# A Hymba layer with sixteen experts on one core: g3 split, the last up product in two banks, one scatter at the end

## The chip, the cores and the metric

The kernel runs on one core of one Trainium2 chip. Its time is device microseconds (us) of that core, taken as the median of several runs. One further execution was recorded by the hardware profiler; the rows below come from it.

## What is computed

One layer for 512 tokens of width 1024, all in float32. An attention part (latent attention and differential attention side by side) comes first; then each token goes to two of sixteen experts, which lie inside one group of four. The change concerns the experts only:

```python
D_MODEL, SEQ, N_EXPERTS, D_EXPERT = 1024, 512, 16, 512
def _hmoe(h, w_rg, b_rg, w_re, b_re, w_gate, w_up, w_down):
    t = h.reshape(B * S, D)
    g_logits = (t @ w_rg + b_rg).astype(jnp.float32)
    g_idx = jnp.argmax(g_logits, axis=-1)
...
    y = jnp.zeros_like(t)
    for e in range(N_EXPERTS):
        he = jax.nn.silu(t @ w_gate[e]) * (t @ w_up[e])
        y = y + gate[:, e:e + 1] * (he @ w_down[e])
    return y.reshape(B, S, D)

...
        x = x + g2 * _hmoe(h2, w_rg[l], b_rg[l], w_re[l], b_re[l], w_gate[l], w_up[l], w_down[l])
```

`gate` holds a token's weight for each expert, zero for those that it did not choose; `h2` is x after normalisation and modulation.

## The kernel before

**Tiles.** Each expert works on 128 slots, filled with the tokens that chose it. Its rows are gathered from DRAM by an indirect DMA on GpSimd's queue (`xg`, line 1602), worked on, weighted by the gate and added to the output by an indirect DMA that adds in DRAM (`scatter`, line 1609). If an expert has more tokens than slots, a second program part, which lies behind a branch, does the rest; it was not entered in the profiled execution.

**Chunks.** An expert's three weight matrices are cut into twelve chunks of 128 partitions x 1024 values: g0 to g3 (gate) and u0 to u3 (up), each with two of the eight k tiles of 128 and 512 columns, and d0 to d3 (down), each one k tile with 1024 columns. The list `CH` sets their order. The gate chunks run one expert ahead: u0 to u3 of expert e, g0 to g3 of e + 1, d0 to d3 of e, and so on. The weights come in loads of 1 MB, two chunks each, into an arena of twelve places (`PLACES`); the next load into a place is issued when both of its chunks are used.

**Split and whole chunks.** Most products take operands of the type fp32r. To keep float32's precision a chunk is split into two such parts four chunks ahead of its use (`AHEAD`): ScalarE casts it to `whi` (line 1579), VectorE takes the rest as `wlo` (line 1580). `mm3` (lines 235 to 237) then adds three products, whi by xh, wlo by xh and whi by xl. A split chunk is six such narrow products of 512 columns. A chunk for which `whole` is true isn't split: it is multiplied in float32 (line 1901), which is two products, recorded as four matmuls, and costs neither ScalarE nor VectorE anything. In the kernel before these are g3 and u3 of each expert. A split normally stands ahead of the products of the chunk four before it; where the table `late_split` names that chunk, it stands behind them.

**Turns.** The gathered rows of an expert have to be transposed. `turn(e, q)`, for half q of the eight k tiles, is four transposes on TensorE (line 1710, into `ps_tp`), four scaled copies `xf` and one cast `xh` on ScalarE (lines 1695 and 1697) and the rest `xl` on VectorE (line 1698). In the kernel before, the first half of expert e stands behind g3 of expert e - 1, which is just ahead of d0 of expert e - 2, and the second behind u0 of expert e - 1. The indirect DMA for expert e + 2's rows is issued behind the second. `turn_act` does the same for the activation: `sl` is the gate through Silu, multiplied by the up product on VectorE (line 1927), transposed on TensorE (line 1870), copied to `he` on ScalarE (line 1873), its rest taken on VectorE (line 1874). It stands behind g1 of the next expert. One expert needs the two turns and one `turn_act`: three times four transposes.

**Slots.** A chain of small steps per expert (`slot_chain`) finds its tokens' row numbers: a one-hot `oh` on VectorE (line 1658), four bf16 products on TensorE, five tiny VectorE operations (lines 1633 to 1640). Numbers in the loop over the chunks say at which chunk each step is issued.

**Order.** The program's order is kept on each engine as it is written; an engine that has to wait holds up all that stands behind it. `take` and `drop` hand out and return buffers.

**The last expert.** Its down products are done for the first 512 output columns, chunk by chunk; those for the second 512 are put off, then made in one go. Each half of `y` has a scatter of its own, over the output seen as half rows, with row numbers `i0` and `i1`. `y` is line 1962: gate, times the PSUM bank `ps_sc`, times the row vector g2.

## Time and profile before

| | us |
|---|---|
| runs | 679.75, 676.32, 678.45 |
| median of the runs | 678.45 |
| the profiled execution's own time | 679.67 |
| its span, first to last instruction | 678.0 |
| TensorE, matmuls (PE) | 639.6 busy, 94% |
| TensorE, weight loads (PEld) | 505.5 busy, 75% |
| VectorE (DVE) | 554.9 busy, 82% |
| ScalarE (ACT) | 433.3 busy, 64% |
| GpSimd (POOL) | 157.9 busy, 23% |

Busy times are shares of the span. Matmuls follow each other in a pipeline, and their ends are modelled: the duration of one matmul is longer than the distance to the next, so TensorE's pace is read from the starts of its instructions. The same holds in part for VectorE, where the start of the next instruction is a little ahead of the recorded end. The expert loop fills the span from about 360 us to its end. The 1.67 us by which the profiled execution's own time exceeds its span lie outside the recorded instructions.

### The profile page before, as it was taken

How to read it: one execution, taken by the hardware profiler on the slowest of the kernel's cores; microseconds unless marked ns; L12 is line 12 of the kernel's file. 1: busy time of each engine (PE TensorE's matmuls, PEld its weight loads, DVE VectorE, ACT ScalarE, POOL GpSimd, SP SyncE). 2: the span in 40 equal slices, each digit the busy share in tenths (PEclk: the TensorE clock that was granted, in tenths of full speed). 3: DMA queues.
4: the chain of work that ended last, by engine and by line, in shares of the span. 5: the costliest groups of instructions: out<-in, count | busy, mean ns of one | idle time of the engine just before them, and what ended most of it. 6: DMA issues, size and time to landing. Idle time of an engine off the chain costs nothing.

```text
span 678.0 us, 10463 instructions
## 1 busy us (share of the span) xinstructions
PE 639.6 (94%) x3465; PEld 505.5 (75%) x3465; DVE 554.9 (82%) x1229; ACT 433.3 (64%) x835; POOL 157.9 (23%) x230
## 2 busy tenths in 40 slices
PE   8998899999989999999999999999999999999991
PEld 7666798998777876767787677777777777777761
DVE  5768887898887677789988888998988888888870
ACT  6575555755664454433477877777787778777750
POOL 2653021266120001132010111222211022231121
...
DMA packets 61931, 169.67 MB, mean 250 GB/s; under 512 B 8807, under 2 KB 23629, under 8 KB 54576
## 3 DMA queue, kind: packets, MB, share of 16 engines
...
q14 instruction: 31, 0.25, 0.1%
...
## 4 chain that ended last, share of the span: by engine, by line
PE 53%; DVE 10%; DMA 3%; ACT 2%; issue 2%; POOL 0%; POOLq 0%; DVEq 0%; ACTq 0%
PE ps_mm L1901 8%; PE ps_mm L235 7%; PE ps_mm L237 7%; PE ps_mm L236 7%; PE ps_sc L235 4%; PE ps_sc L237 4%; PE ps_sc L236 4%; PE ps_tp L1710 2%; DVE acc L1238 2%; DMA xg<-h_d,idx 1%; PE ps_po L887 1%; PE ps_sc L860 1%; PE ps_tp L1870 1%; PE ps_sc L1088 1%; PE ps_tp L874 1%
## 5 line engine op out<-in xcount | busy, mean ns | idle before, releaser
L1580 DVE TENSOR_TENSOR wlo<-wraw,whi 128x1024 fp32r<-128x1024 f32 (+1 forms) x168 | 190.3, 1170 | 8.9 <-ACT whi L1579 8.8
L1579 ACT CAST whi<-wraw 128x1024 fp32r<-128x1024 f32 (+1 forms) x168 | 157.9, 1005 | 0.9 <-PE ps_sc L237 0.5
L1609 POOL DMA_INDIRECT out_dram<-y,idx x15 | 39.9, 2659 | 216.3 <-DVE y L1962 216.3
L235 PE MATMUL ps_mm<-whi,xh 128*128 128x512 f32 x192 | 84.3, 439 | 0.0
L237 PE MATMUL ps_mm<-whi,xl 128*128 128x512 f32 x192 | 75.4, 393 | 0.0
L236 PE MATMUL ps_mm<-wlo,xh 128*128 128x512 f32 x192 | 75.0, 391 | 0.0
L1901 PE MATMUL ps_mm<-wraw,xf 128*128 128x512 f32 x128 | 60.2, 592 | 0.0
L1695 ACT ACTIVATE xf<-ps_tp,norm2x 128x128 f32<-128x128 f32 x120 | 45.1, 462 | 18.2 <-PE ps_tp L1710 18.2
L235 PE MATMUL ps_mm<-whi,hT_hi 128*128 128x256 f32 x192 | 56.7, 295 | 0.0
L236 PE MATMUL ps_mm<-wlo,hT_hi 128*128 128x256 f32 x192 | 55.0, 287 | 0.6 <-DVE wlo L223 0.6
L237 PE MATMUL ps_mm<-whi,hT_lo 128*128 128x256 f32 x192 | 54.8, 285 | 0.0
L235 PE MATMUL ps_sc<-whi,he 128*128 128x512 f32 x128 | 52.8, 412 | 0.7 <-ACT he L1873 0.7
L1238 DVE SCALAR_TENSOR_TENSOR acc<-adaw,s_c,acc 128x512 f32<-128x512 f32 x60 | 47.0, 791 | 4.6 <-DMA adaw<-in_w_ada_dram 3.8
L237 PE MATMUL ps_sc<-whi,he 128*128 128x512 f32 x128 | 50.2, 392 | 0.0
L236 PE MATMUL ps_sc<-wlo,he 128*128 128x512 f32 x128 | 49.9, 390 | 0.0
L236 PEld LDWEIGHTS ps_mm<-wlo,xh 128*128 128x128 f32 x192 | 36.2, 189 | 9.8 <-issue 3.3
L235 PEld LDWEIGHTS ps_mm<-whi,xh 128*128 128x128 f32 x192 | 36.1, 188 | 9.7 <-issue 3.6
L237 PEld LDWEIGHTS ps_mm<-whi,xl 128*128 128x128 f32 x192 | 36.0, 188 | 8.3
L236 PEld LDWEIGHTS ps_mm<-wlo,hT_hi 128*128 128x128 f32 x192 | 37.3, 194 | 1.0 <-DVE wlo L223 0.9
L235 PEld LDWEIGHTS ps_mm<-whi,hT_hi 128*128 128x128 f32 x192 | 37.3, 194 | 0.3
L1873 ACT CAST he<-ps_tp 128x512 fp32r<-128x512 f32 x16 | 9.4, 587 | 43.7 <-PE ps_tp L1870 43.7
L237 PEld LDWEIGHTS ps_mm<-whi,hT_lo 128*128 128x128 f32 x192 | 37.2, 194 | 0.0
...
## 6 DMA issues: line engine op xcount, KB each, us to landing
...
```

The lines of the kernel that those rows point to most:

```text
L235: PE.matmul(o, xh, wh, start=first, stop=False)
L236: PE.matmul(o, xh, wl, start=False, stop=False)
L237: PE.matmul(o, xl, wh, start=False, stop=last)
L860: PE.matmul(s_[:, z * W:(z + 1) * W], qT[h // 4][0:QK + NT, h % 4, qs], kT[h // 4][0:QK + NT, h % 4, 0:W], start=True, stop=True)
L1238: V.scalar_tensor_tensor(acc[0], w[:, z, :], sc, acc[0], op0=OP.mult, op1=OP.add)
L1579: A.copy(hi[:, s], src)
L1580: V.tensor_tensor(lo[:, s], src, f32(hi[:, s]), op=OP.subtract)
L1609: G.indirect_dma_start(out=o, out_offset=bass.IndirectOffsetOnAxis(ap=idx[:, :1], axis=0), in_=y[:, cs], in_offset=None, compute_op=OP.add)
L1695: A.activation(xf[:, kk, :], p3[:, kk, :], AF.Identity, scale=gc, bias=sc)
L1710: PE.transpose(pt[:, kk * P:(kk + 1) * P], xs_["g"][:, e % 2, k0:k0 + P], ident)
L1873: A.copy(xs_["he"][:, 0], p3)
L1901: PE.matmul(eb[nm, e], eb["xf", e][:, 2 * j + kk - 4, :], src, start=(j == 0 and kk == 0), stop=(j == 3 and kk == 1))
```

## The change

`whole` is true for u3 alone: g3 is split like the other chunks, so each expert has eleven split chunks where it had ten. Three tables move with it. `late_split` names u3, d1, g1 and u0. The first turn of expert e stands behind d2 of expert e - 2, three chunks later than before, and the second behind u2 of expert e - 1, two chunks later. The slot chain starts one chunk later, and its last two steps stand two chunks later than before.

For the last expert the up product goes into two PSUM banks of 256 columns each: u0 to u2 as narrow products of 256 columns, u3 as four float32 products of 256. Then each half is multiplied into `sl` (line 1931 of the new kernel), and `turn_act` runs once for each half, with two transposes each. The last expert's down products are made like all others, both halves of the columns chunk by chunk, and one scatter writes whole rows; the row numbers `i0` and `i1` go.

The new kernel's line numbers differ by a few: `oh` is line 1648, the turn's `xl` line 1688, its transposes line 1700, the activation's transposes line 1860, its `he` lines 1864 and 1865, the whole u3 line 1892 and line 1897 for the last expert, the scatter line 1606.

```diff
@@ whole @@
-        return nm + str(j) in ('g3', 'u3')
+        return nm + str(j) in ('u3',)
...
@@ scatter @@
-    def scatter(idx, y, half=None):
-        o, cs = out, slice(0, D)
-        if half is not None:
-            o, cs = out.rearrange("s (h n) -> (s h) n", h=2), slice(half * 512, half * 512 + 512)
-        G.indirect_dma_start(out=o, out_offset=bass.IndirectOffsetOnAxis(ap=idx[:, :1], axis=0), in_=y[:, cs],
+    def scatter(idx, y):
+        G.indirect_dma_start(out=out, out_offset=bass.IndirectOffsetOnAxis(ap=idx[:, :1], axis=0), in_=y[:],
                              in_offset=None, compute_op=OP.add)
...
@@ turn_act @@
-    def turn_act(e):
+    def turn_act(e, lo=0, hi=4):
 
         sl = eb["sl", e]
         pt = take("tp")
-        for kk in range(4):
-            PE.transpose(pt[:, kk * P:(kk + 1) * P], sl[:, kk * P:(kk + 1) * P], ident)
-        drop(sl)
-        p3 = pt.rearrange("p (k n) -> p k n", k=4)
-        A.copy(xs_["he"][:, 0], p3)
-        V.tensor_tensor(xs_["he"][:, 1], p3, f32(xs_["he"][:, 0]), op=OP.subtract)
+        for kk in range(lo, hi):
+            PE.transpose(pt[:, (kk - lo) * P:(kk - lo + 1) * P], sl[:, kk * P:(kk + 1) * P], ident)
+        if hi == 4:
+            drop(sl)
+        p3 = pt[:, 0:(hi - lo) * P].rearrange("p (k n) -> p k n", k=hi - lo)
+        A.copy(xs_["he"][:, 0, lo:hi], p3)
+        V.tensor_tensor(xs_["he"][:, 1, lo:hi], p3, f32(xs_["he"][:, 0, lo:hi]), op=OP.subtract)
         drop(pt)
...
-    late_split = {'u3': 1, 'g2': 1, 'g1': 1, 'd3': 1, 'd1': 1, 'g0': 1}
+
+    late_split = {'u3': 1, 'd1': 1, 'g1': 1, 'u0': 1}
...
@@ the loop over the chunks @@
-            d = c - max(12 * e1 - 38, e1 - 2)
+            d = c - max(12 * e1 - 37, e1 - 2)
             if d == 0:
                 ahead[e1] = slot_chain(e1)
-            for _ in range({0: 3, 3: 1, 4: 1}.get(d, 0)):
+            for _ in range({0: 3, 4: 1, 5: 1}.get(d, 0)):
                 next(ahead[e1], None)
-            if e1 == 2 and d == 4:
+            if e1 == 2 and d == 5:
...
         if whole(nm, j):
             for kk in range(2):
                 src = hi[:, kk * 512:kk * 512 + 512] if hi is lo else (hi, lo)[kk]
-                PE.matmul(eb[nm, e], eb["xf", e][:, 2 * j + kk - 4, :], src, start=(j == 0 and kk == 0), stop=(j == 3 and kk == 1))
+                if (nm, e) != ("u", NE - 1):
+                    PE.matmul(eb[nm, e], eb["xf", e][:, 2 * j + kk - 4, :], src, start=False, stop=(kk == 1))
+            if (nm, e) == ("u", NE - 1):
+                for h, u in enumerate(eb[nm, e]):
+                    for kk in range(2):
+                        src = hi[:, kk * 512:kk * 512 + 512] if hi is lo else (hi, lo)[kk]
+                        PE.matmul(u[:, 0:256], eb["xf", e][:, 2 * j + kk - 4, :], src[:, h * 256:h * 256 + 256], start=False,
+                                  stop=(kk == 1))
...
-                eb[nm, e] = take("mm")
+                eb[nm, e] = [take("mm"), take("mm")] if (nm, e) == ("u", NE - 1) else take("mm")
             for kk in range(2):
                 kt = 2 * j + kk
                 cs = slice(kk * 512, kk * 512 + 512)
+                if (nm, e) == ("u", NE - 1):
+                    for h, u in enumerate(eb[nm, e]):
+                        ch = slice(kk * 512 + h * 256, kk * 512 + h * 256 + 256)
+                        mm3(u[:, 0:256], xs_["h"][:, e % 2, kt, :], xs_["l"][:, e % 2, kt, :], hi[:, ch], lo[:, ch], kt == 0, False)
+                    continue
                 mm3(eb[nm, e], xs_["h"][:, e % 2, kt, :], xs_["l"][:, e % 2, kt, :], hi[:, cs], lo[:, cs], kt == 0, kt == 7)
...
-            for n in range(2) if e + 1 < NE else (0,):
+            for n in range(2):
                 cs = slice(n * 512, n * 512 + 512)
                 mm3(eb["y", e][n], xs_["he"][:, 0, j, :], xs_["he"][:, 1, j, :], hi[:, cs], lo[:, cs], j == 0, j == 3)
-            if e + 1 == NE:
-                last.append((hi, lo))
-        if not whole(nm, j) and (nm, e) != ("d", NE - 1):
+        if not whole(nm, j):
...
-        if (nm, j) == ("u", 3):
+        if (nm, j) == ("u", 3) and e + 1 < NE:
             V.tensor_tensor(eb["sl", e], eb["sl", e], eb["u", e], op=OP.mult)
             drop(eb["u", e])
-            if e + 1 == NE:
-                turn_act(e)
+        elif (nm, j) == ("u", 3):
+            for h, u in enumerate(eb["u", e]):
+                V.tensor_tensor(eb["sl", e][:, h * 256:h * 256 + 256], eb["sl", e][:, h * 256:h * 256 + 256], u[:, 0:256],
+                                op=OP.mult)
+                turn_act(e, 2 * h, 2 * h + 2)
+            drop(*eb["u", e])
         for q in range(2):
-            for e1 in (1,) if e < 1 else (e, e + 1, e + 2):
+            for e1 in (e, e + 1, e + 2):
                 if e1 >= NE or e1 < 1:
                     continue
-                at = ((0, "u", 1 + q)) if e1 == 1 else ((e1 - 1, 'g', 3), (e1 - 1, 'u', 0))[q]
+                at = ((0, "u", 1 + q)) if e1 == 1 else ((e1 - 2, 'd', 2), (e1 - 1, 'u', 2))[q]
...
-                if e + 1 == NE and n:
-                    scatter(slots[e][2], y, 0)
-                    for k, (hi, lo) in enumerate(last):
-                        mm3(eb["y", e][n], xs_["he"][:, 0, k, :], xs_["he"][:, 1, k, :], hi[:, cs], lo[:, cs], k == 0, k == 3)
                 V.scalar_tensor_tensor(y[:, cs], eb["y", e][n], slots[e][1], rows["g2"][:, cs], op0=OP.mult,
                                        op1=OP.mult)
             drop(*eb["y", e])
-            if e + 1 == NE:
-                scatter(slots[e][3], y, 1)
-            else:
-                scatter(slots[e][0], y)
+            scatter(slots[e][0], y)
```

VectorE, one expert in the steady loop, before, from the product `sl` behind u3 on. The `wlo` rows are, in order, those of d0, d1, d2, d3 and of the next expert's u0 to u2; `sv` begins the small slot operations.

```order
L1927 TENSOR_TENSOR sl_6797<-sl_6797,ps_mm_6875 128x512
L1580 TENSOR_TENSOR wlo_6934<-wraw_6596,whi_6933 128x1024
L1874 TENSOR_TENSOR he_5431<-ps_tp_6943,he_5431 128x512
L1580 TENSOR_TENSOR wlo_6951<-wraw_6596,whi_6950 128x1024
L1658 TENSOR_TENSOR oh_6956<-iota_307,rkp 128x512
L1580 TENSOR_TENSOR wlo_6965<-wraw_6614,whi_6964 128x1024
L1580 TENSOR_TENSOR wlo_6969<-wraw_6614,whi_6968 128x1024
L1698 TENSOR_TENSOR xl_5430<-xf_6985,xh_5429 128x512
L1580 TENSOR_TENSOR wlo_6993<-wraw_6661,whi_6992 128x1024
L1580 TENSOR_TENSOR wlo_7016<-wraw_6661,whi_7015 128x1024
L1580 TENSOR_TENSOR wlo_7022<-wraw_6742,whi_7021 128x1024
L1633 COPY sv_1333_7025<-ps_po_7004 128x5
```

The same engine and place in the changed kernel. The `wlo` rows are those of g3, d0, d1, d2, d3 and of u0 to u2.

```order
L1927 TENSOR_TENSOR sl_6861<-sl_6861,ps_mm_6935 128x512
L1580 TENSOR_TENSOR wlo_6991<-wraw_6620,whi_6990 128x1024
L1580 TENSOR_TENSOR wlo_6997<-wraw_6650,whi_6996 128x1024
L1865 TENSOR_TENSOR he_5437<-ps_tp_7013,he_5437 128x512
L1580 TENSOR_TENSOR wlo_7021<-wraw_6650,whi_7020 128x1024
L1580 TENSOR_TENSOR wlo_7027<-wraw_6666,whi_7026 128x1024
L1580 TENSOR_TENSOR wlo_7037<-wraw_6666,whi_7036 128x1024
L1648 TENSOR_TENSOR oh_7042<-iota_307,rkp 128x512
L1580 TENSOR_TENSOR wlo_7053<-wraw_6700,whi_7052 128x1024
L1580 TENSOR_TENSOR wlo_7071<-wraw_6700,whi_7070 128x1024
L1580 TENSOR_TENSOR wlo_7077<-wraw_6798,whi_7076 128x1024
L1688 TENSOR_TENSOR xl_5436<-xf_7091,xh_5435 128x512
```

Behind `sl` two `wlo` stand ahead of `he` where one stood; `oh` stands behind two more of them, and the first half's `xl` has moved from behind d3's `wlo` to behind that of u2.

TensorE at the end of the gate chunks of a steady expert, before: the second half of g2, g3 whole (`x2`), the first turn of the next gathered rows, and d0 with `he`.

```order
L235 MATMUL ps_mm_7642<-whi_7625,xh_5429 128x512
L236 MATMUL ps_mm_7642<-wlo_7626,xh_5429 128x512
L237 MATMUL ps_mm_7642<-whi_7625,xl_5430 128x512
L1901 MATMUL ps_mm_7642<-wraw_7334,xf_7603 128x512 x2
L1710 MATMUL ps_tp_7696<-ident,xg_5312 128x128 x4
L235 MATMUL ps_sc_7712<-whi_7649,he_5431 128x512
L236 MATMUL ps_sc_7712<-wlo_7650,he_5431 128x512
L237 MATMUL ps_sc_7712<-whi_7649,he_5431 128x512
L235 MATMUL ps_sc_7713<-whi_7649,he_5431 128x512
L236 MATMUL ps_sc_7713<-wlo_7650,he_5431 128x512
```

The same place in the changed kernel: the second half of g2, the six products of g3, and the first of d0.

```order
L235 MATMUL ps_mm_7933<-whi_7893,xh_5435 128x512
L236 MATMUL ps_mm_7933<-wlo_7894,xh_5435 128x512
L237 MATMUL ps_mm_7933<-whi_7893,xl_5436 128x512
L235 MATMUL ps_mm_7933<-whi_7923,xh_5435 128x512
L236 MATMUL ps_mm_7933<-wlo_7924,xh_5435 128x512
L237 MATMUL ps_mm_7933<-whi_7923,xl_5436 128x512
L235 MATMUL ps_mm_7933<-whi_7923,xh_5435 128x512
L236 MATMUL ps_mm_7933<-wlo_7924,xh_5435 128x512
L237 MATMUL ps_mm_7933<-whi_7923,xl_5436 128x512
L235 MATMUL ps_sc_7987<-whi_7929,he_5437 128x512
L236 MATMUL ps_sc_7987<-wlo_7930,he_5437 128x512
L237 MATMUL ps_sc_7987<-whi_7929,he_5437 128x512
```

Where the two float32 products stood, six narrow ones stand, and the turn is gone from between g3 and d0.

VectorE from the last expert's d0 on, before: three splits, `sl`, `he`, the last split and the two halves of `y`.

```order
L1580 TENSOR_TENSOR wlo_8223<-wraw_7961,whi_8222 128x1024
L1580 TENSOR_TENSOR wlo_8234<-wraw_7961,whi_8233 128x1024
L1580 TENSOR_TENSOR wlo_8244<-wraw_8030,whi_8243 128x1024
L1927 TENSOR_TENSOR sl_8177<-sl_8177,ps_mm_8226 128x512
L1874 TENSOR_TENSOR he_5431<-ps_tp_8256,he_5431 128x512
L1580 TENSOR_TENSOR wlo_8264<-wraw_8030,whi_8263 128x1024
L1962 SCALAR_TENSOR_TENSOR y_5499<-ps_sc_8267,gate_7745,g_921_5331 128x512
L1962 SCALAR_TENSOR_TENSOR y_5499<-ps_sc_8268,gate_7745,g_921_5331 128x512
```

VectorE at the same place in the changed kernel.

```order
L1580 TENSOR_TENSOR wlo_8359<-wraw_8055,whi_8358 128x1024
L1580 TENSOR_TENSOR wlo_8363<-wraw_8055,whi_8362 128x1024
L1580 TENSOR_TENSOR wlo_8379<-wraw_8096,whi_8378 128x1024
L1931 TENSOR_TENSOR sl_8299<-sl_8299,ps_mm_8344 128x256
L1865 TENSOR_TENSOR he_5437<-ps_tp_8399,he_5437 128x256
L1931 TENSOR_TENSOR sl_8299<-sl_8299,ps_mm_8345 128x256
L1865 TENSOR_TENSOR he_5437<-ps_tp_8405,he_5437 128x256
L1580 TENSOR_TENSOR wlo_8411<-wraw_8096,whi_8410 128x1024
L1962 SCALAR_TENSOR_TENSOR y_5505<-ps_sc_8414,gate_7864,g_921_5331 128x512
L1962 SCALAR_TENSOR_TENSOR y_5505<-ps_sc_8415,gate_7864,g_921_5331 128x512
```

`sl` and `he` come in halves of 256, and the second half's `sl` stands behind the first half's `he`.

## Rows read from the trace of the kernel before

**Rows 1.** Busy us and count per engine in a stretch, PEclk, DMA share, GB/s.

```profile
480.00:500.00 20.00, 20.00 (x92) 15.01 (x91) 17.73 (x24) 15.98 (x25) 4.41 (x2) 1.00 1.02 386
```

**Rows 2.** TensorE's timeline, one expert: start us, us, engine, line, operation, out<-in, count.

```profile
510.19 0.60 PE L1870 MATMUL ps_tp<-ident,sl 128*128 128x128 f32 x4
...
512.01 1.88 PE L1901 MATMUL ps_mm<-wraw,xf 128*128 128x512 f32 x4
513.73 0.60 PE L1710 MATMUL ps_tp<-ident,xg 128*128 128x128 f32 x4
...
522.38 0.40 PE L235 MATMUL ps_mm<-whi,xh 128*128 128x512 f32 x1
...
523.76 0.39 PE L235 MATMUL ps_mm<-whi,xh 128*128 128x512 f32 x1
...
528.94 0.60 PE L1870 MATMUL ps_tp<-ident,sl 128*128 128x128 f32 x4
```

**Rows 3.** VectorE's timeline, one expert; [idle us before <-what ended it].

```profile
548.92 0.69 DVE L1874 TENSOR_TENSOR he<-ps_tp,he 128x512 fp32r<-128x512 f32 x1 [1.08 <-ACT he L1873]
549.87 1.23 DVE L1580 TENSOR_TENSOR wlo<-wraw,whi 128x1024 fp32r<-128x1024 f32 x1 [0.26 <-ACT whi L1579]
551.01 0.69 DVE L1658 TENSOR_TENSOR oh<-iota,rkp 128x512 bf16<-128x512 f32 x1
551.61 2.35 DVE L1580 TENSOR_TENSOR wlo<-wraw,whi 128x1024 fp32r<-128x1024 f32 x2
554.30 0.69 DVE L1698 TENSOR_TENSOR xl<-xf,xh 128x512 fp32r<-128x512 f32 x1 [0.33 <-ACT xh L1697]
555.25 3.50 DVE L1580 TENSOR_TENSOR wlo<-wraw,whi 128x1024 fp32r<-128x1024 f32 x3 [0.26 <-ACT whi L1579]
558.67 0.16 DVE L1633 COPY sv<-ps_po 128x5 f32<-128x5 f32 x1
...
559.34 1.41 DVE L1962 SCALAR_TENSOR_TENSOR y<-ps_sc,gate,g 128x512 f32<-128x512 f32 x2
```

**Rows 4.** ScalarE's timeline, the copies after a turn's transposes.

```profile
552.12 1.50 ACT L1695 ACTIVATE xf<-ps_tp,norm2x 128x128 f32<-128x128 f32 x4
553.65 0.62 ACT L1697 CAST xh<-xf 128x512 fp32r<-128x512 f32 x1
```

**Rows 5.** TensorE's timeline at the start of the expert loop.

```profile
371.47 0.63 PE L1710 MATMUL ps_tp<-ident,xg 128*128 128x128 f32 x4 [0.15 <-DMA xg<-h_d,idx]
```

**Rows 6.** DMA queues from 626.1 us on: packets, MB, share of 16 engines.

```profile
q1 hardware_dynamic: 955, 2.50, 12.3%
```

**Rows 7.** Timeline of all engines around the last expert's activation.

```profile
654.00 1.88 PE L1901 MATMUL ps_mm<-wraw,xf 128*128 128x512 f32 x4
...
656.66 0.66 PE L1870 MATMUL ps_tp<-ident,sl 128*128 128x128 f32 x4 [0.78 <-DVE sl L1927]
657.35 0.58 ACT L1873 CAST he<-ps_tp 128x512 fp32r<-128x512 f32 x1 [4.82 <-PE ps_tp L1870]
...
657.99 0.50 PE L235 MATMUL ps_sc<-whi,he 128*128 128x512 f32 x1 [0.67 <-ACT he L1873]
...
664.06 0.75 DVE L1962 SCALAR_TENSOR_TENSOR y<-ps_sc,gate,g 128x512 f32<-128x512 f32 x1 [1.97 <-PE ps_sc L237]
```

**Rows 8.** TensorE's timeline, narrow products of 256 columns early in the kernel.

```profile
120.10 0.28 PE L235 MATMUL ps_mm<-whi,hT_hi 128*128 128x256 f32 x1
...
120.82 0.28 PE L235 MATMUL ps_mm<-whi,hT_hi 128*128 128x256 f32 x1
```

**Rows 9.** Scatters: GpSimd's timeline; issues (median us to landing); the output's tile.

```profile
668.00 1.55 POOL L1609 DMA_INDIRECT out_dram<-y,i  x1 [4.08 <-DMA out_dram<-y,i]
...
out_dram<-y,idx POOLq DMA_INDIRECT x2, 8.1
...
L1609 POOL DMA_INDIRECT out_dram<-y,idx x1: 4552/4552/4552, 651.7 to 651.7; - x1
...
DMA to landing us min/median/max: 4.8/4.9/9.3
```

16 lines of the change are left out of this document (4 added, 12 removed).

## The prediction

> **What bounds the kernel now.** I read the table of busy times by stretch first, then the timelines of TensorE, VectorE and ScalarE over one expert, then the start and the end of the expert loop. In the loop TensorE is busy 20.00 of 20 us, VectorE 17.73 and ScalarE 15.98 [rows 1]. A busy TensorE need not be the bound, so the test is its spacing. The four transposes of the activation come at 510.19 and at 528.94: one expert takes 18.75 us [rows 2]. A chunk of six narrow products takes 1.38 us (522.38 to 523.76), the chunk left whole takes 1.72 (512.01 to 513.73), a turn of four transposes with the slower product behind it takes 0.44 (510.19 to 512.01 is 1.82, less 1.38) [rows 2]. Ten split chunks, two whole ones and three turns make 13.8 + 3.44 + 1.32 = 18.56; the small slot products fill up to 18.75. So nothing but its own work sets TensorE's pace there. VectorE idles in the same expert 1.08 us before `he`, 0.33 before `xl` and twice 0.26 before `wlo`, all on ScalarE [rows 3]: 1.93 us, so its work is 18.75 - 1.93 = 16.82 us an expert. That engine is second, and near.
>
> **Part 1, g3 split.** TensorE loses the whole chunk and gets a split one: 1.72 - 1.38 = 0.34 us an expert. For expert 0 this is worth nothing: the transposes of expert 1 wait there at 371.47 for the gathered rows to land [rows 5], g3 of expert 0 lies ahead of them in both orders, and nothing on the way to that gather gets earlier. The other 15 experts give 15 x 0.34 = **5.1 us**; with the first one 5.4 would be the most.
>
> The cover has to hold on VectorE: one more `wlo` of 1.14 us an expert (549.87 to 551.01) makes 16.82 + 1.14 = 17.96 us of work. TensorE's new period is 18.75 - 0.34 = 18.41. So VectorE may wait 0.45 us an expert, where it waits 1.93 now, and the question is whether the new order removes these waits. I laid one expert out by hand in the order of the changed program. TensorE, from u0 at 0: u0 to u2 end at 4.14, transposes, u3 from 4.58 to 6.30, g0 and g1 end at 9.06, turn of the activation to 9.50, g3 ends at 12.26, d0 to d2 end at 16.40, transposes at 16.40, d3 ends at about 18.4. ScalarE starts 0.69 us after the first transpose (656.66 to 657.35 [rows 7]) and needs 1.53 + 0.62 us for the copies (552.12 to 553.65, and one `xh`) [rows 4]. So the `xl` of the first half can start at 16.40 + 2.84 = 19.24, which is 0.83 in the next period. From there VectorE runs in order: `xl` to 1.43 (0.60, 551.01 to 551.61), `y` twice to 2.84 (1.41), slot rows to 3.51 (558.67 to 559.34) [rows 3], three `wlo` to 6.93; the second `xl` is ready at 4.14 + 2.84 = 6.98, to 7.58; `sl` to 8.18, where TensorE wants it at 9.06; `wlo` of g3 to 9.32, wanted at 11.1; `wlo` of d0 to 10.46; `he` to 11.06, with ScalarE's `he` ready at 9.06 + 0.69 + 0.59 = 10.34 and TensorE wanting the result at 12.7; d1 waits a little for its cast (about 0.2) and ends at 12.4, wanted at 13.9; d2 13.5, d3 14.7, `oh` 15.3, u0 to u2 18.7; then 0.5 of waiting for the next `xl` at 19.24. What moved is that the `he` wait is gone: two `wlo` stand ahead of it now (g3 and d0) where one stood (d0). The smallest margin is 0.88 us, at `sl`. So I take TensorE as the bound in the loop still, with 0.5 us of air on VectorE. If that air is used up, each further 0.1 us an expert costs 1.5 us.
>
> ScalarE gets a cast of about 1 us an expert on top of 15.98 of 20 us [rows 1] and has room. The weights' queue q1 moves only 2.50 MB after 626.1 us, about 28 us ahead of the first product of the last down matrix at 657.99 [rows 6, 7], so a loop that is 2% faster meets no transfer; g3's place in the arena is even free earlier, at its cast. The moved transposes and slot chains issue the same instructions. Of the moved gather: it stands behind the transposes after u2, no longer u0, and behind the scatter on POOL, and its rows are wanted a whole expert later. No wait is priced there.
>
> **Part 2, the last up in two banks.** The three split chunks become 72 products of 256 columns instead of 36 of 512. Six such products took 120.82 - 120.10 = 0.72 us earlier in the kernel [rows 8], so 72 x 0.12 = 8.64 against 36 x 0.23 = 8.28: **+0.4 us**.
>
> **Part 3, the activation turned in halves.** Before: u3 starts at 654.00, transposes at 656.66, ScalarE at 657.35, first down product at 657.99 [rows 7], 3.99 us after u3's start. After, counted from u3's start: the first half's products are through at about 1.05, VectorE multiplies it to 1.5 beside the second half, transposes come at 1.72, ScalarE copies from about 2.25 to 2.7, VectorE's low half to 3.1. In VectorE's order the product of the second half stands behind that: 3.1 to 3.5. TensorE transposes the second half from 3.6 and starts the down products at about 3.8 without waiting for its copy, since the first two k tiles belong to the first half. That is 0.2 earlier, and the third product does not wait for the low half any more (it did so by about 0.25). I take **-0.45**, bounds -0.9 (no queueing of the second half behind the low half) and +0.3 (down products wait for the second copy).
>
> **Part 4, one scatter.** Before, the last `y` starts at 664.06 and ends at 664.81, but the second half scatter is held until 668.00 by the landing of the first, and lands 4.9 us later at 672.9: 8.1 us after `y` [rows 7, 9]. A whole scatter took 8.1 us as the mean of the last two, 9.3 the slower, so 6.9 the faster, which ran on an otherwise idle queue [rows 9]. With 0.3 of issue: 7.2 after `y`, **-0.9**; with 9.3 it is 9.6, +1.5. I take the faster one, since its descriptors took the usual time on POOL and the other's 4.55 [rows 9]. As the lower bound a whole scatter at a half's price plus its longer descriptors, 5.9: -2.2. Both halves of `y` are written one after the other at the end in either kernel, so the products' reordering costs nothing. The Trainium skill, "DMA: Bandwidth & Descriptors", section "Anatomy of one DMA — SWDGE (gpsimd) path", puts a transfer at about 2.0 us and bytes over 436 GB/s; by that estimate a half takes 2.6 and a whole 3.2 us, the first half would not hold the second, and one scatter would cost 0.6 us more. The trace does not agree: 4.9 us for a half.
>
> **Sum.** -5.1 + 0.4 - 0.45 - 0.9 = -6.05 us. Made against the profiled execution (span 678.0, its own time 679.67) that is 673.6; that run lies 1.2 above the median, and from the median of 678.45 it is **672.4 us**.
>
> **Rivals.**
> A, VectorE becomes the bound: its 17.96 us of work keep the waits for `he` and `xl` (1.08 + 0.33), so that an expert takes 19.37 instead of 18.75. Then 15 x 0.62 = 9.3 more, less 0.95 at the end: 686.8, slower. It decides from 0.79 us of waits an expert on (18.75 - 17.96). For it: VectorE is busy 89% already and the margin is thin. Against it: each wait of now stands where ScalarE had itself waited for TensorE, and the new order has work in these places. The Trainium skill, "Perfetto Trace Analysis", section "Identifying the Most-Contended Engine", takes occupancy as a fair measure for VectorE and not for TensorE. By that rule VectorE is the bound now; worked out from the rows, with 1.14 us added to every expert and nothing hidden, that would be 678.45 + 17.1 - 0.95 = 694.6. The trace does not bear it out: 1.93 us idle on VectorE an expert, and TensorE's period explained by its own work.
> B, the gain is eaten: VectorE waits about 0.8 us an expert in other places (`xl`, `sl`), the period stays at 18.75, and only the end gains: 677.5, no change that can be told.
> C, as forecast, but the one scatter at the price of the slow one: 674.8.
>
> **How the numbers follow.** As forecast 0.55, C 0.13, B 0.17, A 0.12, better than 669.5 0.03. The range holds the forecast's bounds (678.45 - 5.4 - 0.9 - 2.2 + 0.4 = 670.3, a little under it for the medians' spread), C and B: 669.5 to 678.0; A and the better case, 0.15, are left out. A measurement of this kernel tells about 0.5% (3.4 us) from no change: faster is the forecast, C and the better case, 0.71; same is B, 0.17; slower is A, 0.12.
>
> **What would show it.** Right: the activation's transposes on TensorE about 18.4 us apart; VectorE without an idle stretch before `he` and with its wait before the first `xl`; TensorE without waits on VectorE; one scatter within 0.5 us of the last `y`, landing 7 us later. Wrong: TensorE or its weight loads waiting for `wlo` or `sl` once an expert, a period of 18.7 or more, or a last scatter that lands over 9 us after its issue.

## The result and the profile after

The changed kernel takes 667.9 us (median of 4 runs, 667.01 to 671.38) where the kernel before takes 678.72; the ratio is 0.9855, with a 95% interval of 0.9811 to 0.9900. Measured a second time on another occasion it took 668.1 against 678.02, ratio 0.985, interval 0.9831 to 0.9869. So it is faster, by 10.8 us the first time and 9.9 the second. The forecast had the sign right and was too small: 6.05 us, 672.4, and its range ended at 669.5.

To see where the time went I cut both traces at five instructions that both have. "Last x" is the start of the last four transposes of x before the expert loop, "first act" that of expert 0's activation, "last act" that of expert 14's, "u3" that of the last up chunk, "y" the end of the last weighting of the output.

| stretch | before | after | difference | forecast |
|---|---|---|---|---|
| start to last x | 345.35 | 342.73 | -2.62 | 0 |
| last x to first act | 33.32 | 31.81 | -1.51 | 0 |
| first act to last act, 14 experts | 262.22 | 255.99 | -6.23 | -4.76 |
| last act to u3 | 13.11 | 12.94 | -0.17 | +0.06 |
| u3 to y | 10.81 | 10.12 | -0.69 | -0.45 |
| y to the end of the span | 13.19 | 12.11 | -1.08 | -0.9 |

(The forecast's 5.1 us are 15 times 0.34: fourteen times here, and once in the fourth line, with the 0.4 of the narrower products.) The first line cannot be put down to the change. In the fourteen traces of this study the last x lies anywhere from 342.73 to 347.55 us, for the changed kernel itself at 342.73 and 343.44, and for one and the same kernel (e8_sl_first and e8_again below) at 343.25 and 345.91. What moves it is open: TensorE's mean granted clock in the first 50 us was 0.93 in the kernel before and 1.00 in the changed one, but the latest of the fourteen (e4_tail) had 1.00 there too. The next four lines hardly move between executions; the last one moves by up to 0.7 us (11.46 and 12.15 in the two traces of e8). The five sum to -9.7 us, near the 9.9 and 10.8 of the medians.

The loop after the change, in the table of busy times by stretch (stretch, its us, busy us and count of PE, PEld, DVE, ACT, POOL, clock, DMA share, GB/s), answers to [rows 1]:

```profile
480.00:500.00 20.00, 20.00 (x94) 15.42 (x92) 19.50 (x27) 17.25 (x28) 4.72 (x4) 1.00 1.02 385
```

VectorE went from 17.73 to 19.50 busy us of 20. TensorE's timeline over one expert (start us, us, engine line operation), against [rows 2]:

```profile
521.17 0.60 PE L1860 MATMUL ps_tp<-ident,sl 128*128 128x128 f32 x4
...
528.45 0.60 PE L1700 MATMUL ps_tp<-ident,xg 128*128 128x128 f32 x4
528.88 0.24 PE L1652 MATMUL ps_po<-rt,oh 128*128 128x5 bf16 x4
...
534.54 0.60 PE L1700 MATMUL ps_tp<-ident,xg 128*128 128x128 f32 x4
534.98 1.88 PE L1892 MATMUL ps_mm<-wraw,xf 128*128 128x512 f32 x4
...
539.47 0.60 PE L1860 MATMUL ps_tp<-ident,sl 128*128 128x128 f32 x4
```

An expert takes 18.30 us, with no wait on TensorE. The first turn now has the slot products behind it, the second the whole u3. VectorE in the same expert, against [rows 3]:

```profile
520.32 2.35 DVE L1580 TENSOR_TENSOR wlo<-wraw,whi 128x1024 fp32r<-128x1024 f32 x2
522.59 0.68 DVE L1865 TENSOR_TENSOR he<-ps_tp,he 128x512 fp32r<-128x512 f32 x1
523.38 3.50 DVE L1580 TENSOR_TENSOR wlo<-wraw,whi 128x1024 fp32r<-128x1024 f32 x3
526.80 0.68 DVE L1648 TENSOR_TENSOR oh<-iota,rkp 128x512 bf16<-128x512 f32 x1
527.40 3.56 DVE L1580 TENSOR_TENSOR wlo<-wraw,whi 128x1024 fp32r<-128x1024 f32 x4
531.27 0.69 DVE L1688 TENSOR_TENSOR xl<-xf,xh 128x512 fp32r<-128x512 f32 x1 [0.32 <-ACT xh L1687]
```

Of the four waits of [rows 3], 1.93 us an expert, one of 0.32 us is left, ahead of the first `xl`, where the prediction put it. The end, all engines, against [rows 7]:

```profile
643.47 1.89 PE L1897 MATMUL ps_mm<-wraw,xf 128*128 128x256 f32 x8
...
646.02 0.42 DVE L1865 TENSOR_TENSOR he<-ps_tp,he 128x256 fp32r<-128x256 f32 x1 [1.07 <-ACT he L1864]
646.36 0.41 DVE L1931 TENSOR_TENSOR sl<-sl,ps_mm 128x256 f32<-128x256 f32 x1
646.92 0.41 PE L1860 MATMUL ps_tp<-ident,sl 128*128 128x128 f32 x2 [1.34 <-DVE sl L1931]
647.08 0.48 PE L235 MATMUL ps_sc<-whi,he 128*128 128x512 f32 x1
...
652.16 1.43 DVE L1962 SCALAR_TENSOR_TENSOR y<-ps_sc,gate,g 128x512 f32<-128x512 f32 x2 [2.22 <-PE ps_sc L237]
...
653.87 1.54 POOL L1606 DMA_INDIRECT out_dram<-y,idx  x1 [8.01 <-DVEq L1980]
```

From u3 to the first down product 3.61 us (3.99 before), and one scatter 0.3 us behind y. The output's tile says when that scatter lands:

```profile
DMA to landing us min/median/max: 6.6/6.6/6.6
```

6.6 us, against 6.9 and 9.3 for the two whole scatters of [rows 9].

### The profile page after: what moved, and what is told of

Same layout as the page of the kernel before. It is cut to its first block, busy times and chain, and to the rows that moved or that the text cites. A ratio compares the mean times of both kernels' runs of the same rounds, so it can differ in the third digit from the quotient of the medians.

```text
span 665.7 us, 10611 instructions
## 1 busy us (share of the span) xinstructions
PE 628.7 (94%) x3519; PEld 513.2 (77%) x3519; DVE 569.4 (86%) x1244; ACT 450.2 (68%) x852; POOL 142.5 (21%) x229
## 5 line engine op out<-in xcount | busy, mean ns | idle before, releaser
L1580 DVE TENSOR_TENSOR wlo<-wraw,whi 128x1024 fp32r<-128x1024 f32 (+1 forms) x184 | 205.8, 1172 | 2.9 <-ACT whi L1579 1.3
L1579 ACT CAST whi<-wraw 128x1024 fp32r<-128x1024 f32 (+1 forms) x184 | 174.4, 1011 | 0.7 <-PE ps_mm L237 0.4
L235 PE MATMUL ps_mm<-whi,xh 128*128 128x512 f32 (+1 forms) x230 | 96.3, 419 | 0.0
L237 PE MATMUL ps_mm<-whi,xl 128*128 128x512 f32 (+1 forms) x230 | 88.7, 386 | 0.0
L236 PE MATMUL ps_mm<-wlo,xh 128*128 128x512 f32 (+1 forms) x230 | 88.4, 384 | 0.0
L1606 POOL DMA_INDIRECT out_dram<-y,idx x16 | 29.7, 1858 | 226.7 <-DVE rw L1632 174.0
L235 PEld LDWEIGHTS ps_mm<-whi,xh 128*128 128x128 f32 x230 | 43.3, 188 | 11.1 <-issue 3.6
L237 PEld LDWEIGHTS ps_mm<-whi,xl 128*128 128x128 f32 x230 | 43.2, 188 | 9.1
L1602 POOL DMA_INDIRECT xg<-h_d,idx x15 | 23.4, 1562 | 32.8 <-DVE idx L1595 17.2
L867 ACT ACTIVATE p<-ps_sc,nm 128x128 f32<-128x128 f32 (+3 forms) x32 | 16.8, 530 | 19.5 <-DVE nm L864 18.7
```

Of the source, the lines that this page charges most:

```text
L235: PE.matmul(o, xh, wh, start=first, stop=False)
L236: PE.matmul(o, xh, wl, start=False, stop=False)
L237: PE.matmul(o, xl, wh, start=False, stop=last)
L867: A.activation(p[:, z * W:(z + 1) * W], s_[:, z * W:(z + 1) * W], AF.Exp, bias=nm[:, z:z + 1], accum_out=sm[:, h0 + z:h0 + z + 1])
L1579: A.copy(hi[:, s], src)
L1580: V.tensor_tensor(lo[:, s], src, f32(hi[:, s]), op=OP.subtract)
```

## The experiments

Twelve kernels were run. Times are medians, the kernel before of the same chip and hour in brackets; the other columns are the stretches of the table above, from each kernel's trace.

| kernel | time (before) | last x to first act | 14 experts | to u3 | u3 to y | y to end |
|---|---|---|---|---|---|---|
| before | 678.72 | 33.32 | 262.22 | 13.11 | 10.81 | 13.19 |
| changed | 667.9 (678.72) | 31.81 | 255.99 | 12.94 | 10.12 | 12.11 |
| e1_tables | 678.19 (678.73) | 34.23 | 261.45 | 13.11 | 10.78 | 12.77 |
| e2_g3split | 674.0 (678.73) | 32.78 | 258.13 | 12.73 | 10.77 | 12.89 |
| e3_loop | 670.94 (678.73) | 31.88 | 255.99 | 12.70 | 12.39 | 13.10 |
| e4_tail | 676.64 (678.73) | 33.16 | 262.02 | 13.34 | 10.13 | 12.10 |
| e9_load_late | 670.24 (677.9) | 32.74 | 255.97 | 12.94 | 10.12 | 11.33 |
| e6_slots_old | 678.63 (677.9) | 33.14 | 264.78 | 12.94 | 10.12 | 11.86 |
| e5_turn_u0 | 675.09, one run (677.9) | 31.81 | 261.20 | 12.99 | 10.28 | 12.17 |
| e8_sl_first | 667.73 (677.9) | 31.84 | 256.01 | 12.94 | 9.10 | 11.46 |
| after_again | 668.1 (678.02) | 31.87 | 255.99 | 12.94 | 10.12 | 12.04 |
| e8_again | 667.72 (678.02) | 31.78 | 256.00 | 12.94 | 9.12 | 12.15 |
| e12_defer | 667.6 (678.02) | 31.81 | 255.99 | 12.94 | 9.21 | 11.63 |
| e10_two_scatters | 671.65, one run (678.02) | 31.81 | 255.99 | 12.94 | 10.12 | 15.13 |

### The parts one at a time

**e1_tables**: the three tables alone, on the kernel before.

```diff
-    late_split = {'u3': 1, 'g2': 1, 'g1': 1, 'd3': 1, 'd1': 1, 'g0': 1}
+    late_split = {'u3': 1, 'd1': 1, 'g1': 1, 'u0': 1}
...
-            d = c - max(12 * e1 - 38, e1 - 2)
+            d = c - max(12 * e1 - 37, e1 - 2)
...
-            for _ in range({0: 3, 3: 1, 4: 1}.get(d, 0)):
+            for _ in range({0: 3, 4: 1, 5: 1}.get(d, 0)):
...
-                at = ((0, "u", 1 + q)) if e1 == 1 else ((e1 - 1, 'g', 3), (e1 - 1, 'u', 0))[q]
+                at = ((0, "u", 1 + q)) if e1 == 1 else ((e1 - 2, 'd', 2), (e1 - 1, 'u', 2))[q]
```

> The kernel before with the three tables of the change alone: the turns behind d2 and u2, the slot chain one chunk later, the new late_split. g3 stays whole, the last expert stays as it was. Theory N (the new reading of the two traces): an expert takes 0.42 to 0.445 us less in the changed kernel, of which 0.345 is the chunk g3 itself and the rest comes from fewer changes between the narrow products and other kinds of matmul on TensorE (two returns to narrow products fewer, -0.22, and two turns of transposes that stand ahead of another kind, +0.15). With g3 whole the new places of the turns bring nothing by this count: period 18.70 to 18.75 as before. Rival P: the places of the turns are worth the whole 0.1 us an expert by themselves: period 18.65, about 1.5 us less over the loop. For the start of the loop, theory S: TensorE loses about 1 us in expert 0 to the wait for the one-hot of the slot chain, the later slot chain takes it away, and the time to the first activation's transposes, counted from the last transposes of x, falls from 33.3 us by 1 to 1.5. Rival G: the landing of the gathered rows of expert 1 (9.2 us after its issue) is what the start waits for, and nothing is gained. Time: 678.7 by N and G, 677.4 by N and S, 676 by P and S.

678.19 us, ratio 0.9994 (0.9972 to 1.0016). The loop gained 0.77 us, 0.05 an expert: by themselves the new places are worth little, nearer to theory N (at most 0.05) than to P (0.1). The start got 0.9 slower: TensorE arrived early and waited for the gathered rows, as rival G had it, and these landed 10.1 us after their issue where they took 9.2 in the kernel before. TensorE's timeline of this kernel:

```profile
371.58 0.63 PE L1710 MATMUL ps_tp<-ident,xg 128*128 128x128 f32 x4 [1.96 <-DMA xg<-h_d,idx]
```

**e2_g3split**: g3 split, nothing else.

```diff
-        return nm + str(j) in ('g3', 'u3')
+        return nm + str(j) in ('u3',)
```

> The kernel before with g3 split and nothing else: turns, slot chain and late_split in their old places. Theory N: TensorE gains 0.345 us an expert if VectorE keeps up, a period of 18.40 and 5.2 us over fifteen experts; time 673.5. Rival V: in the old order VectorE keeps its waits for he and xl (1.08 and 0.33 us an expert), its 17.96 us of work no longer fit, and the period is 18.75 to 19.4; time 678.7 to 688. In that case the moved tables are what makes the split pay. Start of the loop by theory S: 0.3 less at most, since the slot chain's wait stays.

674.0 us, ratio 0.9928 (0.9901 to 0.9955). Its steady experts take 18.35 to 18.45 us, 0.34 less on average than before, the prediction's main term. Over all fourteen it gains 4.09 and not 4.76, above all because one wait for gathered rows comes in at the first of them:

```profile
382.08 0.66 PE L1710 MATMUL ps_tp<-ident,xg 128*128 128x128 f32 x4 [0.51 <-DMA xg<-h_d,idx]
```

VectorE keeps up in the old order too, so rival V falls. Its waits from 400 to 600 us, about eleven experts (us in total, times, longest):

```profile
DVE xl L1698 <- ACT xh L1697: 3.4, 10, 0.3
DVE wlo L1580 <- ACT whi L1579: 2.8, 11, 0.3
```

The wait for `he` and one of the two for `wlo` are gone with the split alone; the moved tables then only remove the other `wlo` wait. TensorE's timeline, one expert:

```profile
526.43 0.60 PE L1870 MATMUL ps_tp<-ident,sl 128*128 128x128 f32 x4
...
529.64 0.60 PE L1710 MATMUL ps_tp<-ident,xg 128*128 128x128 f32 x4
...
531.47 0.26 PE L1662 MATMUL ps_po<-rt,oh 128*128 128x5 bf16 x4
...
537.15 0.60 PE L1710 MATMUL ps_tp<-ident,xg 128*128 128x128 f32 x4
...
540.36 1.88 PE L1901 MATMUL ps_mm<-wraw,xf 128*128 128x512 f32 x4
...
544.85 0.60 PE L1870 MATMUL ps_tp<-ident,sl 128*128 128x128 f32 x4
```

**e3_loop**: both edits above together, the end as before.

```diff
-        return nm + str(j) in ('g3', 'u3')
+        return nm + str(j) in ('u3',)
...
-    late_split = {'u3': 1, 'g2': 1, 'g1': 1, 'd3': 1, 'd1': 1, 'g0': 1}
+    late_split = {'u3': 1, 'd1': 1, 'g1': 1, 'u0': 1}
...
```

> g3 split and the three tables, the last expert as before: the changed kernel without its new end. Theory N: period 18.29, 6.2 us over fourteen periods; theory S: 1.0 to 1.5 more at the start of the loop; time 671.0. Rival: the end is worth more than its rows show (2 us) and this kernel comes out at 673 or more.

670.94 us, ratio 0.9882 (0.9853 to 0.9910): 7.8 us less, where 671.0 had been expected; the stretches show 1.44 at the start and 6.23 over the loop, as expected (1.0 to 1.5 and 6.2). The two edits are worth more together than apart: 6.23 us over fourteen experts against 4.09 and 0.77. Of the 1.4 between, 0.5 is the wait for rows in e2. In this one trace the end was disturbed. TensorE's granted clock fell to the lower of its two levels, 1.2 GHz, for 3 us after its pause at the activation, which made "u3 to y" 1.6 us longer (busy times by stretch, columns as above):

```profile
650.00:651.00 1.00, 1.00 (x3) 0.72 (x3) 1.00 (x1) 0.00 (x0) 0.00 (x0) 0.50 1.07 213
```

The kernel before, e1 and e2 make the same pause and did not show it, so nothing is concluded from it.

**e4_tail**: the new end alone, on the kernel before (g3 whole, the old tables).

```diff
-                eb[nm, e] = take("mm")
+                eb[nm, e] = [take("mm"), take("mm")] if (nm, e) == ("u", NE - 1) else take("mm")
...
+                turn_act(e, 2 * h, 2 * h + 2)
...
-            for n in range(2) if e + 1 < NE else (0,):
+            for n in range(2):
...
-            if e + 1 == NE:
-                scatter(slots[e][3], y, 1)
-            else:
-                scatter(slots[e][0], y)
+            scatter(slots[e][0], y)
```

> The kernel before with the new end alone: last up in two banks, the activation turned in halves, one scatter; g3 whole and the old tables. By the rows of the changed kernel the end gains 0.4 from the start of u3 to the first down product, 0.3 in the down products and 1.1 in the scatter, and the narrow products of 256 columns cost 0.4: 1.4 us, 677.3. By the prediction 0.95 us. Rival: the scatter lands late (9.3 us, as one whole scatter of the kernel before did) and the end costs 1 us: 679.7. In all four kernels the stage before the expert loop is the same work in the same order: where its end (the last transposes of x, 345.35 us in the trace of the kernel before, 342.73 in that of the changed one) lies 1 to 3 us apart between traces, that part of the difference is no effect of the change.

676.64 us, ratio 0.9962 (0.9947 to 0.9977), 2.1 us less, where 1.4 had been expected; by the trace 1.5: +0.23 to u3, -0.68 from u3 to y, -1.09 behind y. The three sizes are those of the changed kernel, so the end and the loop add up.

### The start of the loop

TensorE needs expert 1's gathered rows there [rows 5]. In every trace the gather is issued 16.7 to 16.8 us behind the last x; its landing differs. In the kernel before, SyncE's queue, GpSimd's and the tile `xg` read:

```profile
357.17 0.38 SPq L1543 DMA_DIRECT2D wraw<-in_w_down_dram  x1
...
360.67 0.98 SPq L1545 DMA_DIRECT2D wraw<-in_w_gate_dram  x2
```

```profile
362.12 1.11 POOL L1602 DMA_INDIRECT xg<-h_d,idx  x1 [17.17 <-DVE idx L1595]
```

```profile
DMA to landing us min/median/max: 9.2/9.2/9.2
```

In the changed kernel, the same three:

```profile
354.53 2.65 SPq L1543 DMA_DIRECT2D wraw<-in_w_down_dram  x2
...
359.58 0.86 SPq L1545 DMA_DIRECT2D wraw<-in_w_gate_dram  x2
```

```profile
359.48 1.11 POOL L1602 DMA_INDIRECT xg<-h_d,idx  x1 [17.16 <-DVE idx L1595]
```

```profile
DMA to landing us min/median/max: 7.2/7.2/7.2
```

With g3 split ahead of the loop its place in the arena comes free there, so SyncE issues a second down load early, which holds back the two gate loads of 1 MB: they are issued behind the gather and no longer ahead of it. The landing took 9.2, 10.1 and 9.1 us in the three kernels with g3 whole (before, e1, e4), 7.4, 7.2 and 7.2 in e2, e3 and the changed one. The gather is not all that TensorE waits for there. In the kernel before it had already waited for the one-hot of the slot chain, ahead of the rows, and in the changed kernel, where the chain stands later, it does not:

```profile
366.27 0.25 PE L1662 MATMUL ps_po<-rt,oh 128*128 128x5 bf16 x4 [0.74 <-DVE oh L1658]
```

To tell the order of the loads from g3 itself:

**e9_load_late**: the changed kernel, g3 split, but its place given back behind its products.

```diff
             V.tensor_tensor(lo[:, s], src, f32(hi[:, s]), op=OP.subtract)
-        raw_next(c)
+        if c != 3:
+            raw_next(c)
...
         if not whole(nm, j):
             drop(hi, lo)
+        if c == 3:
+            raw_next(3)
```

> The changed kernel with one weight load issued later: the load into the place of expert 0's g2 and g3 (a down matrix of expert 1) is issued behind g3's products, where the kernel before issues it, and not at g3's split ahead of the loop. Everything else is the changed kernel. In the three traces with g3 whole (before, tables alone, new end alone) two gate loads of 1 MB are issued in the 1.5 us ahead of the first gather of the loop, and it lands 9.1 to 10.1 us after its issue; in the three with g3 split the down load takes their turn, they are issued 0.1 to 0.3 us behind the gather, and it lands after 7.2 to 7.4. Theory Q: this order of loads is what makes the landing earlier. Then the gather here lands after 9 to 10 us, TensorE waits 1.3 to 2.2 us for it ahead of expert 1's first transposes, and the time is 1.3 to 2.2 above the changed kernel's 667.9. Rival: the landing has another cause; it stays at 7.2 and the time at 667.9.

670.24 us, ratio 0.988 (0.9854 to 0.9906) to before, where the changed kernel has 0.9855 (0.9811 to 0.9900): as times the two can't be told apart. The trace decides: the two gate loads stand ahead of the gather again, the landing takes 8.7 us, and TensorE waits. SyncE's queue, GpSimd, TensorE and the tile `xg`:

```profile
359.89 1.25 SPq L1545 DMA_DIRECT2D wraw<-in_w_gate_dram  x2
```

```profile
361.94 1.11 POOL L1603 DMA_INDIRECT xg<-h_d,idx  x1 [17.15 <-DVE idx L1596]
```

```profile
370.74 0.63 PE L1701 MATMUL ps_tp<-ident,xg 128*128 128x128 f32 x4 [0.71 <-DMA xg<-h_d,idx]
```

```profile
DMA to landing us min/median/max: 8.7/8.7/8.7
```

The start takes 32.74 us, 0.93 more than in the changed kernel; everything behind it is the same up to y, and the last scatter landed after 5.9 us here, so the stretch behind y is 0.8 shorter. That the median lies 2.3 above the changed kernel's, near the 1.3 to 2.2 that I had expected, is chance: the trace shows less. Theory Q holds, with a smaller landing than its 9 to 10 us and a wait of 0.71. What happens inside the DMA engines between the two queues is not shown by any run.

**e6_slots_old**: the changed kernel with the slot chain's old numbers.

```diff
-            d = c - max(12 * e1 - 37, e1 - 2)
+            d = c - max(12 * e1 - 38, e1 - 2)
...
-            for _ in range({0: 3, 4: 1, 5: 1}.get(d, 0)):
+            for _ in range({0: 3, 3: 1, 4: 1}.get(d, 0)):
...
-            if e1 == 2 and d == 5:
+            if e1 == 2 and d == 4:
```

> The changed kernel with the slot chain in its old place (one chunk earlier, its last steps two chunks earlier). Theory S: in expert 0 TensorE waits again about 0.74 us for the one-hot, and the first activation's transposes lie 32.6 to 32.8 us behind the last transposes of x where the changed kernel has 31.8 (0.9 lost). In the loop the slot products stand by themselves again and not behind the first turn's transposes: by the segments of the two traces a lone turn and lone slot products take 0.655 us, together 0.63, so 18.29 becomes 18.32 to 18.35, 0.4 to 0.8 us over the loop. Together 669.2 to 669.6. Rival: the slot chain's place costs nothing, 667.9, and the start's gain is the gather's landing alone.

678.63 us, ratio 1.0005 (0.9993 to 1.0016): the whole gain is gone. The start loses 1.3 us to the one-hot, where theory S had 0.9. The surprise is the loop: 18.97 to 19.04 us an expert, where I had expected 18.35. TensorE and VectorE of this kernel, one expert:

```profile
535.86 0.26 PE L1652 MATMUL ps_po<-rt,oh 128*128 128x5 bf16 x4 [0.52 <-DVE oh L1648]
```

```profile
541.63 0.69 DVE L1688 TENSOR_TENSOR xl<-xf,xh 128x512 fp32r<-128x512 f32 x1 [0.57 <-ACT xh L1687]
...
547.57 0.69 DVE L1688 TENSOR_TENSOR xl<-xf,xh 128x512 fp32r<-128x512 f32 x1 [0.52 <-ACT xh L1687]
```

TensorE waits 0.52 us for `oh`, which stands behind the splits on VectorE; its transposes come later, so ScalarE's `xh`, so VectorE waits 1.09 us for both halves. The waits close a ring: neither engine sets the pace alone. VectorE's work and its waits fill the 19.04 us (the prediction's 17.96 and 1.09 are 19.05), and TensorE's own work, without the hold at `oh`, would take 18.36 us, near the 18.35 that I had expected: the product ahead of the slot products starts at 534.95, 0.91 us before them, where the others follow each other at 0.23. This is the kind of loss that rival A of the prediction described, at other places.

**e5_turn_u0**: the changed kernel with the second turn behind u0.

```diff
-                at = ((0, "u", 1 + q)) if e1 == 1 else ((e1 - 2, 'd', 2), (e1 - 1, 'u', 2))[q]
+                at = ((0, "u", 1 + q)) if e1 == 1 else ((e1 - 2, 'd', 2), (e1 - 1, 'u', 0))[q]
```

> The changed kernel with the second turn back behind u0, two chunks earlier, where narrow products follow it; in the changed kernel the whole u3 follows. Theory N: by the segments of the two traces four transposes with narrow products behind them take 0.36 us and 0.12 more at the first narrow product, ahead of the whole chunk 0.44 and nothing more: 0.04 us an expert, period 18.33 instead of 18.29. Rival V: VectorE loses its order, since the second half's low part then stands ahead of two splits, and TensorE waits once an expert: 18.5 or more.

675.09 us in one run; a steady expert takes 18.61 to 18.69 us, as rival V had it. VectorE and TensorE, one expert:

```profile
540.03 0.69 DVE L1688 TENSOR_TENSOR xl<-xf,xh 128x512 fp32r<-128x512 f32 x1 [0.66 <-ACT xh L1687]
540.98 3.50 DVE L1580 TENSOR_TENSOR wlo<-wraw,whi 128x1024 fp32r<-128x1024 f32 x3 [0.26 <-ACT whi L1579]
```

```profile
544.66 0.39 PE L237 MATMUL ps_mm<-whi,xl 128*128 128x512 f32 x1
545.13 0.66 PE L1860 MATMUL ps_tp<-ident,sl 128*128 128x128 f32 x4
```

The second `xl` comes to VectorE's front before ScalarE has its input: 0.92 us of waits, 17.7 us of work. So VectorE is late with `sl`, and TensorE is held once an expert: 0.47 us from the last narrow product to the transposes of `sl`, where it is 0.23 in the changed kernel, and these transposes take 0.41 instead of 0.35. Without these 0.30 us an expert would take 18.34: by the rows theory N's 18.33 for the turn's place on TensorE holds too, though no time shows it alone.

### The end

**after_again**, the changed kernel without an edit, and **e8_sl_first** with its repetition **e8_again**: both halves of `sl` ahead of the first low part of `he`.

```diff
             for h, u in enumerate(eb["u", e]):
                 V.tensor_tensor(eb["sl", e][:, h * 256:h * 256 + 256], eb["sl", e][:, h * 256:h * 256 + 256], u[:, 0:256],
                                 op=OP.mult)
+            for h in range(2):
                 turn_act(e, 2 * h, 2 * h + 2)
```

> The changed kernel unaltered, beside the two versions of its end on the same chip. 667 to 668.5. Its trace shows again whether the stage before the loop varies between executions (the last transposes of x have lain between 342.7 and 347.6 us so far) while the loop does not: period 18.29, 31.8 us from the last transposes of x to the first activation's.

> The changed kernel with two VectorE instructions of the last expert exchanged: both halves of the up product are multiplied into the activation before the low part of the first half is taken. Theory T: in the changed kernel the second half's product waits behind the first half's low part (646.02 to 646.36, which itself waits for ScalarE), so its transposes start at 646.92, and TensorE reaches the first down product at 647.08. With the exchange the second product runs at 645.1 to 645.5, the transposes at 645.6, the first down product at about 646.0: 1.0 us less, 666.9. Rival: the down products wait for the second half anyway, or VectorE's wait only moves: 0 to 0.3 less.

> The exchange of the second half's product and the first half's low part again, now beside the changed kernel itself on the same chip. In its first trace the end took 9.10 us from the start of u3 to the end of y, 10.12 in the changed kernel: 1.0 us less is expected of the time. Rival: the gain is below what the runs can show, ratio 1.000.

The trace of the second, all engines:

```profile
648.56 0.42 DVE L1931 TENSOR_TENSOR sl<-sl,ps_mm 128x256 f32<-128x256 f32 x1 [0.44 <-PE ps_mm L1897]
...
649.04 0.44 PE L1860 MATMUL ps_tp<-ident,sl 128*128 128x128 f32 x2 [0.30 <-DVE sl L1931]
...
649.24 0.48 PE L235 MATMUL ps_sc<-whi,he 128*128 128x512 f32 x1
```

From u3 (646.63) to the first down product 2.61 us instead of 3.61, and from u3 to y 9.10 and 9.12 instead of 10.12 twice: the queueing behind the low part cost 1.0 us in the changed kernel. The medians, 667.73 and 667.72 against 667.9 and 668.1, show 0.2 to 0.4 of it, less than the spread of the stage before the loop; as a time the gain cannot be told.

**e12_defer**: the same, with the last expert's second 512 columns multiplied after the first, and the last split earlier.

```diff
-            for n in range(2):
+            for n in range(2) if e + 1 < NE else (0,):
...
-                turn_act(e, 2 * h, 2 * h + 2)
...
+            for k, src in enumerate(parts):
+                A.copy(dh[:, k * n:k * n + n], src)
+            turn_act(e, 0, 2)
+            for k, src in enumerate(parts):
+                V.tensor_tensor(dl[:, k * n:k * n + n], src, f32(dh[:, k * n:k * n + n]), op=OP.subtract)
+            turn_act(e, 2, 4)
...
+                if e + 1 == NE and n:
+                    for k, (hi, lo) in enumerate(last):
+                        mm3(eb["y", e][n], xs_["he"][:, 0, k, :], xs_["he"][:, 1, k, :], hi[:, cs], lo[:, cs], k == 0, k == 3)
```

> The exchange of the run above, and two things more in the last expert: the down products of the second 512 columns are made after those of the first, as in the kernel before, but still with one scatter; and the last down chunk is cast ahead of the activation's copies, its rest taken between the two low parts. Theory: in the changed kernel both halves of y stand behind the last product (652.16 to 653.59, the last product starts at 652.41); with the first half of y made earlier only one is left: 0.5 to 0.6 us less than the exchange alone, 1.5 less than the changed kernel. Rival: the chunk order makes TensorE wait for the last chunk's rest, and the gain is gone.

667.6 us, and 9.21 us from u3 to y where the exchange alone has 9.12: no gain. My theory was wrong. The first half of y in the changed kernel starts at 652.16, before the last product (652.41), since its bank is complete three products earlier. The end of y lies 1.18 us behind the start of the last product there and 1.17 in e12, so there was nothing to win, and the down products took 0.1 us longer (5.44 from the first start to the last, 5.33 in the changed kernel).

**e10_two_scatters**: the changed kernel with two half scatters.

```diff
...
+                if e + 1 == NE:
+                    scatter(slots[e][2 + n], y, n)
             drop(*eb["y", e])
-            scatter(slots[e][0], y)
+            if e + 1 < NE:
+                scatter(slots[e][0], y)
```

> The changed kernel with two half scatters at the end as before, each behind its half of y. Theory: the second is held by the first's landing, 5.6 us after the first's issue (662.37 to 668.00 before), and lands 4.9 later; both halves of y end within 0.8 us here, so the landing comes 9.9 us after the last y, where the one scatter takes 7.0: 2.9 us more than the changed kernel. Rival: two halves cost what they did before, 8.1, 1.1 more.

671.65 us in one run, and 15.13 us from y to the end where the changed kernel has 12.11. GpSimd's timeline:

```profile
654.57 1.55 POOL L1609 DMA_INDIRECT out_dram<-y,i  x1 [7.33 <-DVE y L1972]
659.99 1.55 POOL L1609 DMA_INDIRECT out_dram<-y,i  x1 [3.87 <-DMA out_dram<-y,i]
```

The second is held for 5.4 us by the first, as before, but now nothing hides the first: 3.0 us more, as forecast. The new product order and the single scatter belong together.

## Why the prediction was right or wrong

**Right.** TensorE bounds the loop, the split of g3 is worth 0.34 us an expert (e2), and VectorE covers it: the waits for `he` and `wlo` are gone and one of 0.32 us for the first `xl` is left. That two `wlo` stand ahead of `he` was the right reason for the first, and it comes with the split itself: e2, in the old order, has no wait for `he` either. "If that air is used up, each further 0.1 us an expert costs 1.5 us" is what e5 and e6 did: 0.37 and 0.63 us an expert over the changed kernel, 5.2 and 8.8 us over fourteen. The Trainium skill, "Perfetto Trace Analysis", section "Identifying the Most-Contended Engine", takes occupancy as a fair measure for VectorE. The trace after does not bear that out as a bound: 19.50 of 20 us busy, and TensorE still without a wait. Part 4 came out at 1.1 for 0.9, with the landing of 6.6 just under the faster of the two rows that I weighed; the landing varied between traces of kernels with one scatter from 5.9 to 6.7. None of the rivals happened in the changed kernel.

**Wrong: "For expert 0 this is worth nothing."** This step of part 1 is the first miss, 1.5 us. I had seen that the transposes wait there for the gather, which e1 confirms, and then wrote that "nothing on the way to that gather gets earlier". Its issue does not get earlier; its landing does, by 2 us, because the place that g3 gives back earlier changes the order of the weight loads (e9: 0.93 us of the 1.5). I had written that the place is free earlier, and had not followed what SyncE then issues, and when. The rest needs the tables: with the landing early and the slot chain in its old place TensorE still waits for the one-hot (0.74 us in e2, 1.30 in e6; the start gains 0.54 us in e2, and 0.18 in e6). I had read only the wait for the rows, 0.15 us, and not the 0.74 for the one-hot ahead of it. With both waits gone g3's 0.34 counts for expert 0 as well.

**Wrong: the size of the period, 18.41 for 18.29.** The mechanism was right, and TensorE's own work was mis-sized. The second miss, 1.5 us over the loop, is in "a turn of four transposes with the slower product behind it takes 0.44", used alike wherever the turn stands, and in giving the slot products no place: "the moved transposes and slot chains issue the same instructions" put their new neighbours at nothing. The starts in the timelines of e2 (18.42 us in the expert shown) and of the changed kernel (18.30) allow a count. In e2 four groups of other matmuls stand alone between narrow products ahead of u3, and u3 itself: five returns to narrow products. In the changed kernel there are three, because the slot products stand behind the first turn and u3 behind the second. By the distances of the starts, the 66 narrow products of an expert with their returns take 15.93 us in e2 and 15.65 in the other, and the transposes, slot products and u3 take 2.49 and 2.65. That is 0.12 us less. It is read from rows, and the rows of two more kernels bear it out: e5 and e6 have four returns, and with their one hold of TensorE taken off their 66 narrow products take 15.8 us, between the two. No time shows it alone, since in both VectorE's waits come on top.

**Mis-sized at the end.** The products of 256 columns cost 0.23 to 0.24 instead of 0.4 (e4 against before, the changed kernel against e3). The price of each was right, the count was not: three chunks of six products are 18 of 512 columns and 36 of 256, where part 2 has 36 and 72. The rows between d3's last product and u3 show 36 and 18:

```profile
639.15 0.28 PE L235 MATMUL ps_mm<-whi,xh 128*128 128x256 f32 x1
```

```profile
649.92 0.39 PE L235 MATMUL ps_mm<-whi,xh 128*128 128x512 f32 x1
```

The first is the changed kernel, 4.32 us ahead of u3 (643.47); the second the kernel before, 4.08 ahead (654.00 in [rows 7]): 0.24 more. The activation in halves gave 0.69 instead of 0.45: the laid-out order was right, 0.38 us of it lie ahead of the first down product (3.61 us behind u3, where I had 3.8) and 0.31 behind it (where I had 0.25). The cause that I named for its not being more, the second half's queueing behind the first low part, is confirmed by e8, at 1.0 us. One reading was off without effect: from 626.1 us it is 28 us to the last u3, and 32 to the first product of the last down matrix.

**The range.** Its lower bound allowed 5.4 us for the loop, as if 0.34 could only shrink. The bounds on the end reached far below, those of the loop and of its start not at all, and there the time was.
